# Placing the tiles that the dense matmuls read at multiples of 512 bytes of SBUF

## The chip, the core and the metric

The kernel runs on one core of one Trainium2 chip. The metric is the device time of one execution in microseconds (us), from the start to the end of the program on that core. In the profile the engines are called PE (TensorE, the matmuls), PEld (TensorE's loads of the stationary operand), DVE (VectorE), ACT (ScalarE), POOL (GpSimd) and SP (SyncE, which issues most of the DMAs).

A matmul here has a **moving** operand, which streams through the array column by column (up to 512 columns), and a **stationary** operand of 128 x 128, which is loaded ahead of it. In the rows of the trace `mm<-hH,wh` means: output tile `mm`, moving operand `hH`, stationary operand `wh`.

## The reference, cut to what matters

Two layers over 512 tokens with a model width of 1024, everything in float32:

```python
for layer in range(DEPTH):                     # DEPTH = 2
    h = rmsnorm(x, attn_norm[layer])
    proj = einsum('bsd,dc->bsc', h, w_in[layer])       # 6920 columns
    out_a = spatial_gating(...)                # 128 x 128 mixing matrices
    out_b = sliding_window_attention(...)      # 8 heads, window 128, rotary tables
    out_c = gated_deltanet(...)                # chunked recurrence, 4 heads
    merged = sum(sigmoid(gate_i) * (branch_i @ w_branch[layer, i]))   # 3 branches
    x = x + merged @ w_out[layer]
    h2 = rmsnorm(x, ffn_norm[layer])
    gu = h2 @ w_gate_up[layer]                 # 5632 columns
    x = x + (silu(gu[:2816]) * gu[2816:]) @ w_down[layer]
return rmsnorm(x, final_norm)
```

Nearly all the arithmetic is in the products with `w_in`, `w_branch`, `w_out`, `w_gate_up` and `w_down`. These are called the dense matmuls below. The rest (delta rule, attention, transposes) is made of many small matmuls.

## The kernel before

**Number format.** Each float32 operand of a dense matmul is split into a high part, rounded to the matmul format float32r, and a low part, the exact rest. A product is the sum of three matmuls: high x high, high x low, low x high. So there are tiles in pairs: `wh`, `wl` (weights), `hH`, `hL` (normed residual), `brH`, `brL` (branch outputs), `mH`, `mL` (merged branches), `aH`, `aL` (activations of the feed-forward). Each holds 4 bytes for every element.

**Weights.** `wload` fetches 512 KB of weights by DMA into `st` (two buffers), ACT rounds them into `wh`, DVE subtracts to get `wl` (three buffers each). One such load feeds 24 matmuls.

**Dense matmuls.** `fm_acc` takes a slice of 128 columns of `wh` or `wl` as the stationary operand and a whole tile of 512 columns of `hH`, `aH`, `brH` or `mH` (or the low part) as the moving one. `tm_group` has it the other way round: a slice of 128 columns of `hH` or `hL` is stationary and 512 columns of `wh` or `wl` move (264 columns for the projection of attention's keys and values, `wkv`).

**Order.** The class `Issue` writes the order of PE's instructions by a rough clock of its own: the dense matmuls form one long stream, and steps of the delta rule, attention and so on are put between them. The other engines' instructions are ordered by the scheduling layer. The function `layer` goes through key/value projection, the projections of the mixers with the delta rule and attention interleaved, gates and branches, the output projection, and the feed-forward (first gate and up: `hH`, `hL`; then down: `aH`, `aL`).

**Placement.** SBUF is handed out by pools, one after the other in each partition: `const` (constants such as `ones`, `ident`, masks), `lay` (small tiles of a layer), `base` (`hH`, `hL`, five scratch pages `rot`, `ms`, `rst`, `rep`), `wst` (`st`, `wh`, `wl`), and then the pools of the mixers (`mix`, pages of 2 KB) or of the feed-forward (`ffn`). Sizes are rounded up to 32 bytes. A tile's address is therefore the sum of all that stands ahead of it. As the program is built, these are the places of the operands, as the remainder of the address by 512 bytes:

| operands | pool | before | changed |
|---|---|---|---|
| `hH`, `hL` (8 tiles of 2 KB each) | `base` | 96 | 0 |
| `wh`, `wl` (3 buffers of 4 KB each) | `wst` | 224 | 0 |
| `aH`, `aL` | `ffn` | 224 | 0 |
| `brH`, `brL`, `mH`, `mL` | `mix` | 224 | 0 |
| the second half of the 264-wide weights | `wst` | 256 | 32 |
| `ones`, `ident`, `tri_le` | `const` | 288 | 64 |
| `dg` (in `rot`) | `base` | 96 | 0 |

The slices of 128 columns start at multiples of 512 bytes inside their tiles, so a slice has the remainder of its tile.

Of the kernel before, what the change touches and what calls it, by code (L numbers as in the profile page):

```python
# [10 lines left out]
F32 = mybir.dt.float32  # L11
# [7 lines left out]
P = 128  # L19
# [11 lines left out]
# chunk indices of the packed input projection  # L31
# [7 lines left out]
DENSE = 10  # L39
ORDER = "k z qv0 qv1 aq gv u"  # L40
# [7 lines left out]
class Issue:  # L48
    """Merges streams of work into one order for the tensor engine.

    A stream is a generator: it yields None where other streams may go on, or the name of an event to wait for.
    Of the streams whose last step should be through, the one of the lowest rank goes on.  When a step is
    through comes from a rough clock (us): every engine works off what it is given, and waits for operands."""
# [40 lines left out]
    def bank_free(self, tag, n):  # L94
        """when the next of the n banks of this tag can be written"""
        used = self.banks.setdefault(tag, [])
        return self.read.get(used[-n], 0.0) if len(used) >= n else 0.0
# [6 lines left out]
    def front(self, nc):  # L104
        """nc with engines that keep the clock"""
        issue = self

        class Engine:
            def __init__(self, name):
                self.name, self.eng = name, getattr(nc, name)  # L110

            def __getattr__(self, op):
                f = getattr(self.eng, op)

                def call(*args, **kw):
                    issue.note(self.name, op, args, kw)
                    return f(*args, **kw)  # L117

                return call

        class Front:
            vector, scalar, gpsimd, tensor, sync = (Engine(e) for e in ("vector", "scalar", "gpsimd", "tensor", "sync"))

        return Front
# [37 lines left out]
def hybrid_kernel(ctx, tc, x0, pos, wi, wkv, wb, wo, wg, wd, gn, convw, lngb, sguw, sgub,  # L162
# [20 lines left out]
    def pg(tag, name, shape=(P, T), dt=F32):  # L183
        """a page of 2 KB of the layer's pool; a tag's pages are handed out in program order"""
        return pools["mix"].tile(list(shape), dt, tag=tag, name=nm(name), bufs=PAGES[tag])
# [14 lines left out]
    def wload(src, n=1024, ahead=True):  # L200
        """f32 weights -> (high, low) parts, high rounded to float32r and low the exact rest"""
        st = wst.tile([P, 1024], F32, tag="st", name=nm("st"), bufs=2)
        hi = wst.tile([P, 1024], F32R, tag="wh", name=nm("wh"))
        lo = wst.tile([P, 1024], F32R, tag="wl", name=nm("wl"))
        issue.ahead = ahead
        with tc.high_priority() if ahead else nullcontext():
            nc.sync.dma_start(st[:, :n], src)
            nc.scalar.copy(hi[:, :n], st[:, :n])
            nc.vector.tensor_tensor(lo[:, :n], st[:, :n], hi[:, :n].bitcast(F32), ALU.subtract)
        issue.ahead = False  # L210
        return hi, lo

# [1 line left out]
    xp = tc.tile_pool(name="x0", bufs=1, reuse_waits="tile")  # L214
    x0p = xp.__enter__()
    gnt = cst([P, 2 * DEPTH + 1, KT], "gnt")
    nc.sync.dma_start(gnt, gn)
# [19 lines left out]
    # rows p, columns f  # L237
    ident = tri("ident", [[1, P]], 0, -1, ALU.is_equal)
    tri_le = tri("tri_le", [[1, P]], 0, -1, ALU.is_ge)      # f >= p
    tri_gt = tri("tri_gt", [[-1, P]], 0, 1, ALU.is_gt)      # p > f  # L240

    # blk[b][p, f] = 1 when p and f lie in one block of size b
# [11 lines left out]
    # lmt[b][i, j] = 1 when i and j share a block of 2b, j in its left half and i in its right one  # L254
# [7 lines left out]
    # additive masks of the attention band, columns [previous chunk | this chunk]  # L262
# [18 lines left out]
    def rope_tables():  # L281
        with tc.tile_pool(name="rope", bufs=1) as rp:
# [7 lines left out]
            ang = rp.tile([P, NCH, 8], F32, name="ang")  # L290
# [18 lines left out]
            w = rp.tile([P, NCH, 8], F32, name="w")  # L309
# [6 lines left out]
    def fm_acc(ps, w, off, xs, first, last):  # L316
        """ps[c, t] += sum over the k tiles of w[:, off + 128 i ...].T @ xs[i], operands as (high, low)"""
        wh, wl = w
        for i, (xh, xl) in enumerate(xs):
            sl = slice(off + i * P, off + (i + 1) * P)  # L320
            nc.tensor.matmul(ps, lhsT=wh[:, sl], rhs=xh, start=first and i == 0, stop=False)
            nc.tensor.matmul(ps, lhsT=wh[:, sl], rhs=xl, start=False, stop=False)
            nc.tensor.matmul(ps, lhsT=wl[:, sl], rhs=xh, start=False, stop=last and i == len(xs) - 1)
            yield
# [7 lines left out]
    def tm_group(srcs, width, xs):  # L332
        """four banks [128 tokens, width]: tokens by columns, k tiles in pairs; weights may be loaded already"""
        yield issue.bank_free("mm", 1)
        banks = [mm_bank() for _ in range(NCH)]
        for j, src in enumerate(srcs):
            wh, wl = src if isinstance(src, tuple) else wload(src, 2 * width)
            for c in range(NCH):
                tk = slice(c * P, (c + 1) * P)
                for kk in range(2):  # L340
                    xh, xl = xs[2 * j + kk]
                    sl = slice(kk * width, (kk + 1) * width)
                    o = banks[c][:, :width]
                    nc.tensor.matmul(o, lhsT=xh[:, tk], rhs=wh[:, sl], start=j == 0 and kk == 0, stop=False)
                    nc.tensor.matmul(o, lhsT=xh[:, tk], rhs=wl[:, sl], start=False, stop=False)
                    nc.tensor.matmul(o, lhsT=xl[:, tk], rhs=wh[:, sl], start=False, stop=j == 3 and kk == 1)
                yield
        return banks

# [6 lines left out]
    class Norm:  # L356
        """takes the residual tile by tile; gives the scaled operand in two parts and 1/rms"""

        def __init__(self, gi, final=False, split=KT - 1):
            """the squares of the tiles before split are added on GpSimd, the others on VectorE"""  # L360
# [25 lines left out]
        def finish(self):  # L386
# [4 lines left out]
            ms = base.tile([P, NCH], F32, tag="ms", name=nm("ms"), bufs=2)  # L391
            nc.vector.tensor_scalar(ms, ps[:, :NCH], 1.0 / D, EPS, ALU.mult, ALU.add)
            self.rst = base.tile([P, NCH], F32, tag="rst", name=nm("rst"), bufs=2)
# [16 lines left out]
    def layer(l, norm, first=None):  # L410
# [39 lines left out]
        # beta = sigmoid, g = -exp(a_log) * softplus(a + dt_bias)  # L450
# [26 lines left out]
        # 2 z (1 + p) + max(x, 0)  # L477
# [21 lines left out]
        def dn_conv(which, h, name):  # L499
            """2 silu(conv(projection)), feature-major"""  # L500
# [33 lines left out]
        class Delta:  # L534
            """two heads of the gated delta rule, in steps that leave the order of issue to the caller"""
# [15 lines left out]
            def decay(self):  # L551
                """decay^T[j, i] = exp(sum of g over (j, i]) for i >= j"""
# [16 lines left out]
            def keys(self):  # L569
                """scaled k k^T and token-major keys"""  # L570
# [35 lines left out]
            def queries(self):  # L606
                """scaled q k^T, size of q, token-major values"""
# [36 lines left out]
            def solve(self, c):  # L644
                """U = (I + L)^-T by doubling of the diagonal blocks; Tm = U^T"""
# [55 lines left out]
            def scan(self):  # L701
                yield f"z{l}"
                for c in range(NCH):
# [5 lines left out]
                    # right side minus what the state holds already  # L709
# [42 lines left out]
                    # rms norm over the head, z gate  # L752
# [14 lines left out]
        def blocks(wk):  # L767
            """inverses of the 16 x 16 diagonal blocks of I + L, one block a partition"""
# [18 lines left out]
            # [(block, row), inverse or its transpose, (group, chunk, head), column]  # L787
# [8 lines left out]
        def gelu2(x):  # L796
            """x <- 2 gelu(x)"""
# [6 lines left out]
        def sgu_params():  # L804
            """causal mixing matrices and, per column c and row t, lnb[c] * sum_s W[t, s] + b[t]"""
# [30 lines left out]
        def sgu():  # L836
            """us <- 4 u * (W n + b), n the norm of v"""
# [44 lines left out]
        def rope(t, co, si, n, name):  # L882
            """t [P, n, 64], tables [P, n, 8]"""
# [8 lines left out]
        def attn_prep():  # L892
            """keys, then the queries chunk by chunk, feature-major"""
# [31 lines left out]
        def attn_pair(qk, qT, kT, c, a, jj):  # L925
            """two heads of key head a in chunk c; the result replaces the queries"""
# [53 lines left out]
        def to_branch(key, srcs, tags, events):  # L980
            """token-major pieces [feature tile][chunk] -> feature-major (high, low) tiles"""
# [198 lines left out]
def _tiles_fm(w):  # L1180
    """[K, C] -> [C/128, 128, K] : per 128 columns, partition p holds (k tile, column)"""
    K, C = w.shape
    return w.reshape(K // P, P, C // P, P).transpose(2, 1, 0, 3).reshape(C // P, P, K)


def _tiles_tm(w):
    """[K, C] -> [K/256, 128, 2 C]"""
# [66 lines left out]
```

## Time and profile before

| | |
|---|---|
| device time, median of 3 runs | 1800.73 us (1800.56 to 1803.62) |
| span of the profiled execution, first to last instruction | 1798.6 us |
| PE busy in the profiled execution | 1768.7 us of the span (98%) |
| PEld, DVE, ACT, POOL busy | 1451.9, 886.1, 634.7, 399.2 us |
| mean granted TensorE clock | 0.996 of full speed |

The page of the profile gives no time of the profiled execution other than its span, so the median is 2.1 us above it. Matmuls overlap in the array: one that the rows show as 0.39 us long is followed by the next after 0.23 us, so the distance from start to start is what a matmul costs PE, and the length in the row is not.

### The profile page before, as it was taken

How to read it: one execution, taken by the hardware profiler on the slowest of the kernel's cores; microseconds unless marked ns; L12 is line 12 of the kernel's file. 1: busy time of each engine (PE TensorE's matmuls, PEld its weight loads, DVE VectorE, ACT ScalarE, POOL GpSimd, SP SyncE). 2: the span in 40 equal slices, each digit the busy share in tenths (PEclk: the TensorE clock that was granted, in tenths of full speed). 3: DMA queues.
4: the chain of work that ended last, by engine and by line, in shares of the span. 5: the costliest groups of instructions: out<-in, count | busy, mean ns of one | idle time of the engine just before them, and what ended most of it. 6: DMA issues, size and time to landing. Idle time of an engine off the chain costs nothing.

```text
span 1798.6 us, 22123 instructions
## 1 busy us (share of the span) xinstructions
PE 1768.7 (98%) x8458; PEld 1451.9 (81%) x8458; DVE 886.1 (49%) x1756; ACT 634.7 (35%) x1155; POOL 399.2 (22%) x399
## 2 busy tenths in 40 slices
PE   7999999999999999999999999999999999999996
PEld 6888878888888888888888888888888888888885
DVE  7695775454443333333267858654444433333222
ACT  6454454322333222222244435432223322222221
POOL 4413111011223333310043121010222233333011
PEclk9999999999999999999999999999999999999998
DMA  4232112222352222234332311122234522223331
GB/s 156 96 97 72 36 36 77 94 94 94 108 170 97 97 96 94 94 115 134 114 104 93 100 48 36 54 82 94 84 104 135 187 94 94 94 94 93 96 97 65
DMA packets 55784, 171.84 MB, mean 96 GB/s; under 512 B 8000, under 2 KB 8256, under 8 KB 55680
## 3 DMA queue, kind: packets, MB, share of 16 engines
q1 hardware_dynamic: 54432, 167.04, 28.5%
q0 software_dynamic: 1248, 3.41, 0.7%
q8 instruction: 66, 1.08, 0.3%
q14 instruction: 38, 0.31, 0.1%
HBM read 159.41 MB, written 11.01 MB: 95 GB/s over the span
## 4 chain that ended last, share of the span: by engine, by line
PE 96%; DVE 2%; ACT 1%; issue 0%; POOL 0%; DMA 0%; DVEq 0%; SPq 0%; POOLq 0%; ACTq 0%
PE mm L117 85%; PE px L117 10%; DVE wl L117 0%; DVE xf L117 0%; DVE U L117 0%; DMA st<-in_wkv 0%; ACT wh L117 0%; POOL of L117 0%; DVE zg L117 0%; DVE sq L117 0%; DVE ys L117 0%; DVE Tm L117 0%; ACT sq L117 0%; POOL rst L117 0%; DVE hL L117 0%
## 5 line engine op out<-in xcount | busy, mean ns | idle before, releaser
L117 ACT CAST wh<-st 128x1024 fp32r<-128x1024 f32 (+2 forms) x288 | 295.8, 1027 | 814.3 <-PE mm L117 733.4
L117 PE MATMUL mm<-hH,wh 128*128 128x512 f32 x1344 | 538.3, 401 | 0.0
L117 PE MATMUL mm<-hH,wl 128*128 128x512 f32 x1344 | 530.4, 395 | 0.0
L117 PE MATMUL mm<-hL,wh 128*128 128x512 f32 x1344 | 530.2, 394 | 0.0
L117 DVE TENSOR_TENSOR wl<-st,wh 128x1024 fp32r<-128x1024 f32 (+2 forms) x288 | 355.2, 1233 | 184.3 <-ACT wh L117 174.4
L117 PEld LDWEIGHTS mm<-hH,wl 128*128 128x128 f32 x1344 | 252.9, 188 | 59.4
L117 PEld LDWEIGHTS mm<-hH,wh 128*128 128x128 f32 x1344 | 253.2, 188 | 58.5 <-issue 2.7
L117 PEld LDWEIGHTS mm<-hL,wh 128*128 128x128 f32 x1344 | 253.3, 188 | 56.5 <-issue 0.7
L117 PE MATMUL mm<-aH,wh 128*128 128x512 f32 x352 | 137.0, 389 | 0.0
L117 PE MATMUL mm<-aH,wl 128*128 128x512 f32 x352 | 137.0, 389 | 0.0
L117 PE MATMUL mm<-aL,wh 128*128 128x512 f32 x352 | 136.9, 389 | 0.0
L117 POOL TENSOR_TENSOR gt<-gt,gt 128x512 f32<-128x512 f32 x32 | 48.9, 1528 | 306.8 <-DVE gt L117 306.8
L117 POOL TENSOR_TENSOR s<-s,rep 128x512 f32<-128x512 f32 x44 | 77.3, 1756 | 167.5 <-ACT s L117 167.5
L117 POOL TENSOR_TENSOR aL<-s,aH 128x512 fp32r<-128x512 f32 x44 | 76.5, 1738 | 163.4 <-ACT aH L117 163.4
L117 PE MATMUL mm<-wh,hH 128*128 128x512 f32 (+1 forms) x256 | 101.9, 398 | 7.2 <-ACT hH L117 7.2
L117 DVE TENSOR_TENSOR s<-mm,s 128x512 f32<-128x512 f32 x44 | 30.4, 692 | 155.6 <-PE mm L117 148.8
L117 DVE TENSOR_TENSOR s<-mm,rep 128x512 f32<-128x512 f32 x44 | 30.4, 692 | 143.9 <-PE mm L117 140.0
L117 PE MATMUL mm<-wh,hL 128*128 128x512 f32 (+1 forms) x256 | 95.3, 372 | 0.7 <-DVE hL L117 0.4
L117 PE MATMUL mm<-wl,hH 128*128 128x512 f32 (+1 forms) x256 | 94.8, 370 | 0.0
L117 POOL TENSOR_TENSOR sq<-sq,sq 128x512 f32<-128x512 f32 x27 | 40.7, 1509 | 236.3 <-ACT sq L117 236.2
L117 DVE TENSOR_TENSOR gt<-mm,rep 128x512 f32<-128x512 f32 x48 | 33.1, 690 | 103.7 <-PE mm L117 103.7
L117 PEld LDWEIGHTS mm<-aH,wh 128*128 128x128 f32 x352 | 66.1, 188 | 13.9
(250 smaller groups left out, 2359.0 us busy)
## 6 DMA issues: line engine op xcount, KB each, us to landing
st<-in_wi SPq DMA_DIRECT2D x104, 512.0 KB, 3.2
st<-in_wg SPq DMA_DIRECT2D x88, 512.0 KB, 3.3
st<-in_wd SPq DMA_DIRECT2D x32, 512.0 KB, 3.5
st<-in_wb SPq DMA_DIRECT2D x24, 512.0 KB, 3.3
st<-in_wo SPq DMA_DIRECT2D x16, 512.0 KB, 3.4
xscr<-xt SPq DMA_DIRECT2D x24, 256.0 KB, 2.0
st<-in_wd SPq DMA_DIRECT2D x16, 384.0 KB, 3.1
xt<-xscr SPq DMA_DIRECT2D x16, 256.0 KB, 2.7
```

What stands on the lines that cost most here:

```text
L117: return f(*args, **kw)
```

## The change

Five edits, all of placement:

- a tile `pad` of 72 floats (288 bytes) is put into `const` behind `gnt`; nothing reads or writes it;
- `ms` and `rst` (two buffers of 16 bytes each, 32 with rounding) move from `base` to `lay`, ahead of `base`;
- in the rotary tables `ang` is the tile `inv` itself, and `w` is the tile `nh`, which gives up two small tiles at the end of SBUF.

With these the pool `base` starts at 25600 (before: 25184) and `wst` with the weights at 78848 for `wh` (before: 78560), both multiples of 512. The comments and docstrings of the file are left out too, which moves the line numbers by a few.

```diff
+PAD = 72
...
     gnt = cst([P, 2 * DEPTH + 1, KT], "gnt")
+    cst([P, PAD], "pad")
...
             inv = rp.tile([P, NCH, 8], F32, name="inv")
...
-            ang = rp.tile([P, NCH, 8], F32, name="ang")
+            ang = inv
             nc.vector.tensor_tensor(ang, inv, pf.unsqueeze(2).broadcast_to([P, NCH, 8]), ALU.mult)
...
-            w = rp.tile([P, NCH, 8], F32, name="w")
+            w = nh
...
-            ms = base.tile([P, NCH], F32, tag="ms", name=nm("ms"), bufs=2)
+            ms = lay.tile([P, NCH], F32, tag="ms", name=nm("ms"), bufs=2)
             nc.vector.tensor_scalar(ms, ps[:, :NCH], 1.0 / D, EPS, ALU.mult, ALU.add)
-            self.rst = base.tile([P, NCH], F32, tag="rst", name=nm("rst"), bufs=2)
+            self.rst = lay.tile([P, NCH], F32, tag="rst", name=nm("rst"), bufs=2)
```

On each of the five engines the built program has the same instructions in the same order with the same waits as before; only tile names (`inv` for `ang`, `nh` for `w`) and addresses differ.

## Rows read from the trace of the kernel before

**Rows 1.** The page: span, busy time of the engines, chain that ended last.

```profile
span 1798.6 us, 22123 instructions
...
PE 1768.7 (98%) x8458; PEld 1451.9 (81%) x8458; DVE 886.1 (49%) x1756; ACT 634.7 (35%) x1155; POOL 399.2 (22%) x399
...
PE 96%; DVE 2%; ACT 1%; issue 0%; POOL 0%; DMA 0%; DVEq 0%; SPq 0%; POOLq 0%; ACTq 0%
```

**Rows 2.** Waits: who <- for whom: us in total, times, longest us.

```profile
ACT wh L117 <- PE mm L117: 733.4, 230, 6.7
...
PE mm L117 <- ACT hH L117: 7.2, 2, 5.7
PE px L117 <- DVE sq L117: 3.6, 2, 2.4
```

**Rows 3.** PE's timeline in gate and up, layer 0: start us, length us, instruction.

```profile
639.67 0.40 PE L117 MATMUL mm<-hL,wh 128*128 128x512 f32 x1
...
641.05 0.40 PE L117 MATMUL mm<-hL,wh 128*128 128x512 f32 x1
641.30 0.40 PE L117 MATMUL mm<-hH,wl 128*128 128x512 f32 x1
...
641.76 0.39 PE L117 MATMUL mm<-hL,wh 128*128 128x512 f32 x1
```

**Rows 4.** PE's timeline in the down projection, layer 0.

```profile
819.62 0.39 PE L117 MATMUL mm<-aH,wh 128*128 128x512 f32 x1
...
821.66 0.39 PE L117 MATMUL mm<-aH,wh 128*128 128x512 f32 x1
```

**Rows 5.** PE's timeline in the z projection, layer 0 (weights move).

```profile
55.24 0.39 PE L117 MATMUL mm<-wh,hL 128*128 128x512 f32 x1
...
57.10 0.39 PE L117 MATMUL mm<-wl,hH 128*128 128x512 f32 x1
```

**Rows 6.** Groups by operation and form: xcount, busy us, mean ns, idle before.

```profile
L117 PE MATMUL mm<-hH,wh 128*128 128x512 f32 x1344 | 538.3, 401 | 0.0
...
L117 PE MATMUL mm<-aH,wh 128*128 128x512 f32 x352 | 137.0, 389 | 0.0
...
L117 PE MATMUL mm<-wh,hH 128*128 128x512 f32 x192 | 81.8, 426 | 0.0
...
L117 PE MATMUL mm<-brH,wh 128*128 128x512 f32 x192 | 74.8, 389 | 0.0
...
L117 PE MATMUL mm<-mH,wh 128*128 128x512 f32 x128 | 49.8, 389 | 0.0
...
L117 PE MATMUL mm<-wh,hH 128*128 128x264 f32 x64 | 20.1, 314 | 7.2 <-ACT hH L117 7.2
```

**Rows 7.** PE's timeline around a full float32 matmul: x2 is its two passes.

```profile
538.19 1.02 PE L117 MATMUL px<-dg,ones 128*128 128x512 f32 x2
```

**Rows 8.** The tile `dg`: duration ns min/median/max of its matmuls.

```profile
L117 PE MATMUL px<-dg,ones x10: 592/593/1192, 26.3 to 1786.8; 128*128 128x512 f32 x10
```

**Rows 9.** PE's timeline in the first projection, 264 columns, near the program's start.

```profile
9.84 0.42 PE L117 MATMUL mm<-wh,hH 128*128 128x264 f32 x1
...
12.26 0.42 PE L117 MATMUL mm<-wh,hL 128*128 128x264 f32 x1
```

**Rows 10.** PE's timeline in the same projection some microseconds later.

```profile
18.93 0.29 PE L117 MATMUL mm<-wl,hH 128*128 128x264 f32 x1
...
20.14 0.28 PE L117 MATMUL mm<-wh,hL 128*128 128x264 f32 x1
```

**Rows 11.** Stretches: bounds, length, engines' busy us (xcount), clock, DMA share, GB/s.

```profile
150.00:250.00 100.00, 98.50 (x648) 82.43 (x647) 73.36 (x275) 49.23 (x149) 20.61 (x36) 1.00 0.13 43
560.00:740.00 180.00, 180.00 (x776) 145.97 (x775) 61.46 (x65) 51.42 (x64) 58.08 (x33) 1.00 0.29 94
1000.00:1150.00 150.00, 146.60 (x886) 121.05 (x887) 109.89 (x378) 72.26 (x212) 26.07 (x41) 1.00 0.17 54
```

**Rows 12.** Groups in the stretch 150 to 250 us.

```profile
L117 PE MATMUL mm<-wh,hH 128*128 128x512 f32 x40 | 17.4, 436 | 0.0
...
L117 PE MATMUL mm<-hH,wh 128*128 128x512 f32 x12 | 5.3, 440 | 0.0
```

## The prediction

> **What bounds the kernel now.** I read the page first: PE is busy for 98% of a span of 1798.6 us, and 96% of the chain that ended last is PE [rows 1]. The view of waits says the same from the other side: ACT waits 733.4 us in total until PE gives a weight buffer back, while PE's longest sums of waiting are 7.2 and 3.6 us [rows 2]. So weights are never late in the long stretches, and the time is the number of matmuls times the distance from one start to the next. That distance is what the timeline gives; the lengths in its rows overlap.
>
> There are three distances for a dense matmul of 512 columns, all at a granted clock of 1.00, the level of 2.4 GHz [rows 11]. In gate and up (moving `hH`, stationary `wh`) nine steps take 641.76 - 639.67 = 2.09 us, 232.2 ns each [rows 3]. In the down projection (moving `aH`, stationary `wh`) nine take 2.04 us, 226.7 ns each [rows 4]. In the z projection (moving `wh`, stationary `hH`) eight take 1.86 us, 232.5 ns each [rows 5]. The array's own need is 512 / 2.4 = 213.3 ns. So each dense matmul pays 13 to 19 ns on top. The instruction is the same in all three; what differs is where the operands lie. `hH` is at remainder 96 by 512, all other dense operands at 224. Two operands at 224: 226.7. One at 96, in either role: 232.
>
> **What the surplus is not.** It is no fixed cost of a matmul. In the first projection, 264 columns wide, eleven steps near the start take 2.42 us, 220.0 ns each [rows 9]. That is exactly 264 / 1.2, so I read it as the lower level of the clock, with nothing on top, with the same operands and the same weight loads. Later the same matmuls go at 1.21 / 10 = 121.0 ns [rows 10] where 264 / 2.4 is 110.0. A full float32 matmul takes two cycles a column: its two passes start 1.02 - 0.59 = 0.43 us apart [rows 7, 8], where 1024 cycles are 426.7 ns, though its moving tile `dg` is also at 96. So the surplus appears only where one 4-byte element a cycle is asked for at 2.4 GHz: the read of the operands limits, not the array.
>
> The sizes suggest how. 226.7 ns are 544 cycles = 17 x 32. If a read comes in lines of 128 bytes (32 elements, 32 cycles each), 2048 bytes that start at remainder 96 of 128 touch 17 lines and not 16. The 264 columns (1056 bytes) touch 9 lines, 288 cycles, 120.0 ns: the row says 121.0. Lines of 64 bytes would give 33 x 16 = 528 cycles, 220 ns, too little; lines of 256 bytes 9 x 64 = 576, 240 ns, too much. This is an estimate from four spacings, not something that a row shows directly. The 5.5 ns more for a pair at 96 and 224 would then be the two reads getting in each other's way.
>
> A rule of the Trainium skill stands against a part of this. The page "TensorE: Matmul & The Clock Gate", section "Step-by-step: what each phase is for", says that PE reads the moving and the stationary operand by two independent ports, so that loading the next weights takes nothing from the running matmul. By that rule the z projection, whose moving operand is at 224, should go at the 226.7 ns of the down projection; its row says 232.5, so here the measurement decides, and the place of the stationary operand counts too.
>
> **The change part by part.** No instruction, wait or DMA is added, removed or moved; `pad` is never touched. The shared tiles of the rotary tables are some 20 operations of 32 elements on DVE, in the order as before: nothing. `ms` and `rst` are four elements wide: nothing. The sum is therefore the number of dense matmuls times the change of their spacing.
>
> The new spacing at remainder 0: 16 lines are 512 cycles, 213.3 ns, and the fixed part that the float32 pair shows (430 against 426.7 ns) adds 3. I take 216. The bounds are 213.3 (nothing fixed left) and 226.7 (the best that a row shows for this instruction). The value is nearer the lower end because both float32 passes and the slow stretch come within 3 ns of the array's need as soon as the reads aren't the limit.
>
> - Gate, up, gates of branches, and the projections with moving `hH`, `hL`: 3 x 1344 = 4032 matmuls [rows 6], 16.2 ns each: 65.3 us.
> - Projections with moving weights: 3 x 192 = 576, 16.5 ns each: 9.5 us.
> - Moving `aH`, `brH`, `mH` and their low parts: 3 x (352 + 192 + 128) = 2016, 10.7 ns each: 21.6 us.
> - The 264-wide ones: 3 x 64 = 192. At 0 and 32 they still touch 9 lines; 121 to 120 ns, taken as nothing. At most 192 x 8 = 1.5 us.
>
> Together 96.4 us. Against it: in 150 to 250 us and in 1000 to 1150 us PE is idle for 1.5 and 3.4 us [rows 11], between steps of the delta rule and attention that wait for other engines. There dense matmuls fill the waits, and faster ones fill less. About 3 x (40 + 12) = 156 of them lie in the first stretch [rows 12], 156 x 16 = 2.5 us, and by length 3.7 us in the second. I take half of these 6 us as given back: 3 us (bounds 0 and 6). In the feed-forward nothing else comes near: in 180 us DVE works 61, ACT 51, POOL 58, and the DMAs are at a share of 0.29 [rows 11]. At 216 ns for 232 that grows by 7%. If this cover were gone, the next late thing would be `wl`, which DVE makes out of `st`.
>
> The span becomes 1798.6 - 96.4 + 3 = 1705.2 us. The median of the runs is 2.1 us above the profiled span, so 1707 us.
>
> **The rivals.**
>
> 1. *Only the pair counts.* What the rows show directly is that equal remainders do better than unequal ones. If the other 13 ns belong to any full-rate read (544 cycles could also be 512 plus one stolen cycle for each 16 bytes of a 512-byte weight load), all dense matmuls go at 226.7: 4032 x 5.5 + 576 x 5.8 = 25.5 us, 1775 us. For it: it needs nothing that no row has shown. Against it: 264 columns would then need 264 + 32 = 296 cycles, 123.3 ns, and the row says 121.0.
> 2. *Placement does nothing.* `hH` differs from the others also in when it runs and where in SBUF it lies, and that could be the cause; then 1801 us. Against it: `wh` and `hH` swapped give the same spacing. The Trainium skill's page "SBUF — State Buffer" has a rule by which this would be so: "Operand start alignment" asks only for a multiple of the element size (and says that it speaks of legality, not of speed), and "Specifications (TRN2)" gives lines of 16 bytes; every tile here starts at a multiple of 32 before the change. By that the three spacings should be one; the rows have two, 5.5 ns apart.
> 3. *Slower.* With all operands at 0 the moving read and the weight load, which begins as a matmul starts, begin at the same place of a line and of any interleave. If that makes them collide each time, every dense matmul takes what the worst step in gate and up takes, 641.30 - 641.05 = 0.25 us, say 240 ns: 4032 x 7.8 + 576 x 7.5 + 2016 x 13.3 = 63 us more, 1863 us. It decides from a mean spacing of 230.6 ns on, today's mean over all 6624. Against it: two operands at 224 begin alike too, and are the fastest.
> 4. *In between*, the line effect for the moving operand alone with some collisions left, spacing about 221: some 65 us, 1736 us.
>
> **How the numbers follow.** My forecast 0.55, rival 1 0.20, rival 2 0.10, rival 3 0.10, rival 4 0.05. The forecast's own range is 1689 (213.3 ns, 18 us less) to 1727 (219 ns). To leave out no more than 2 in 10 the range has to reach to rival 1: 1689 to 1778. Differences under 0.2% can't be told from none. Faster holds the forecast and rivals 1 and 4: 0.80; the same 0.10; slower 0.10.
>
> **What would show it.** In the changed kernel's timeline, steps of 216 ns in gate and up, down and z alike; if down stays at 226.7 and gate and up comes to it, it is rival 1. The 264-wide steps should stay at 120 to 121 and the float32 pair at 0.43. PE's idle time in the two delta stretches should grow by no more than some 3 us each. I am wrong if the 13 ns at equal remainders don't depend on the place, or if remainder 0 brings collisions of its own.

## The result, and the profile after

The changed kernel takes 1778.83 us (median of 4 runs, 1778.37 to 1779.13), the kernel before 1800.67 us in the same series. The ratio is 0.9875 (95% interval 0.9861 to 0.9889): 1.2% faster, 22 us and not the 94 us that I forecast. The time lies 0.8 us outside my range, next to rival 1 (only the pair counts, 1775 us).

The page of the changed kernel, its span, busy times and chain, as in [rows 1]:

```profile
span 1776.7 us, 22123 instructions
...
PE 1747.9 (98%) x8458; PEld 1451.2 (82%) x8458; DVE 885.9 (50%) x1756; ACT 633.8 (36%) x1155; POOL 397.3 (22%) x399
...
PE 96%; DVE 2%; ACT 1%; issue 0%; POOL 0%; DMA 0%; DVEq 0%; SPq 0%; POOLq 0%; ACTq 0%
```

The same instructions, the other engines as busy as before to within 2 us, PE 21 us less. So only what a matmul costs PE has changed. PE's timeline in gate and up, layer 0, to be held against [rows 3] (start us, length us, instruction):

```profile
639.64 0.39 PE L118 MATMUL mm<-hH,wh 128*128 128x512 f32 x1
...
641.91 0.39 PE L118 MATMUL mm<-hL,wh 128*128 128x512 f32 x1
```

Ten steps in 2.27 us, 227.0 ns; before they were 232.2. In the down projection, against [rows 4]:

```profile
819.61 0.39 PE L118 MATMUL mm<-aH,wl 128*128 128x512 f32 x1
...
821.65 0.39 PE L118 MATMUL mm<-aH,wl 128*128 128x512 f32 x1
```

Nine steps in 2.04 us, 226.7 ns, as before to the digit, although all its operands went from remainder 224 to 0. The full float32 pair, against [rows 7], is unchanged too:

```profile
533.34 1.02 PE L118 MATMUL px<-dg,ones 128*128 128x512 f32 x2
```

The long pieces of the chain that ended last say it for whole stages (start us, length us, what). This is the feed-forward of layer 1, gate and up and then down, before (first line) and now:

```profile
1424.13 356.07 PE mm L117 x1545
...
1408.09 350.25 PE mm L118 x1545
```

That is 230.5 ns a matmul before and 226.7 now.

### The profile page after: what moved, and what is told of

Same layout as the page of the kernel before. It is cut to its first block, busy times and chain, and to the rows that moved or that the text cites. A ratio compares the mean times of both kernels' runs of the same rounds, so it can differ in the third digit from the quotient of the medians.

```text
span 1776.7 us, 22123 instructions
## 1 busy us (share of the span) xinstructions
PE 1747.9 (98%) x8458; PEld 1451.2 (82%) x8458; DVE 885.9 (50%) x1756; ACT 633.8 (36%) x1155; POOL 397.3 (22%) x399
## 4 chain that ended last, share of the span: by engine, by line
PE 96%; DVE 2%; ACT 1%; issue 0%; POOL 0%; DMA 0%; DVEq 0%; SPq 0%; POOLq 0%; ACTq 0%
PE mm L118 86%; PE px L118 10%; DVE wl L118 0%; DVE xf L118 0%; DVE U L118 0%; DMA st<-in_wkv 0%; ACT wh L118 0%; POOL of L118 0%; DVE zg L118 0%; DVE sq L118 0%; DVE Tm L118 0%; DVE ys L118 0%; ACT hH L118 0%; ACT pr L118 0%; ACT sq L118 0%
## 5 line engine op out<-in xcount | busy, mean ns | idle before, releaser
L118 PE MATMUL mm<-hH,wh 128*128 128x512 f32 x1344 | 532.2, 396 | 0.0
L118 PE MATMUL mm<-hH,wl 128*128 128x512 f32 x1344 | 524.0, 390 | 0.0
L118 PE MATMUL mm<-hL,wh 128*128 128x512 f32 x1344 | 523.3, 389 | 0.0
```

## The experiments

Two theories at the start. **Theory 1**: a dense matmul is slow when its two operands have different remainders, and the place itself is of no account. **Theory 2**: the place counts, a multiple of 128 or 512 is good. Spacings below are from start to start in PE's timeline of the run named.

**Each half of the change alone.** The first kernel moves `ms` and `rst` and leaves the pad out, so that every operand lies at 224; the second has the pad and leaves `ms` and `rst` where they were, so that `hH`, `hL` lie at 384 and the rest at 0.

```diff
 # e1_move_only: the changed kernel without
-    cst([P, PAD], "pad")
 # e2_pad_only: the changed kernel with
-            ms = lay.tile([P, NCH], F32, tag="ms", name=nm("ms"), bufs=2)
+            ms = base.tile([P, NCH], F32, tag="ms", name=nm("ms"), bufs=2)
-            self.rst = lay.tile([P, NCH], F32, tag="rst", name=nm("rst"), bufs=2)
+            self.rst = base.tile([P, NCH], F32, tag="rst", name=nm("rst"), bufs=2)
```

> The change without its pad: ms and rst in the layer's pool, so that all operands of the dense matmuls lie at remainder 224 by 512, none at 0. Theory 1 (only the pair counts: what matters is that the moving and the stationary operand have the same remainder): every dense matmul at 226.7 ns, time as the changed kernel, 1779 us. Theory 2 (the place itself counts: a multiple of 512, or of 128, is what helps): the gate and up projection doesn't come down to 226.7, and the time lies above 1785 us, up to 1801.

Measured: 1778.92 us, ratio 0.9879 (0.9864 to 0.9894). Gate and up:

```profile
639.74 0.39 PE L117 MATMUL mm<-hH,wh 128*128 128x512 f32 x1
...
641.78 0.39 PE L117 MATMUL mm<-hH,wh 128*128 128x512 f32 x1
```

Nine steps in 2.04 us, 226.7 ns, with every operand at 224.

> The change with its pad alone (ms and rst back ahead of the weights): hH and hL at remainder 384, weights and all other operands at 0, every one a multiple of 128; the difference of the pair is 128 as in the kernel before. Theory 1 (pair): gate and up stay at 232 ns, the rest at 226.7, time as before, 1801 us. Theory 2 (place): all operands are at multiples of 128, so 226.7 everywhere and 1779 us.

Measured: 1801.33 us, ratio 1.0001 (0.9992 to 1.0011). Gate and up:

```profile
639.74 0.39 PE L118 MATMUL mm<-hL,wh 128*128 128x512 f32 x1
...
641.83 0.39 PE L118 MATMUL mm<-hL,wh 128*128 128x512 f32 x1
```

Nine steps in 2.09 us, 232.2 ns, as in [rows 3], with every operand at a multiple of 128. Theory 1 stands, theory 2 has fallen: the whole gain comes from moving `ms` and `rst`, which takes 128 bytes out from between `hH` and the weights. The pad, which brings the multiples of 512, does nothing. (Both kernels keep the shared tiles of the rotary tables; the second shows that these give nothing either.)

**Which differences cost.** In the feed-forward's own pool gaps can be put between the activations, so that one run holds six differences between moving and stationary operand.

```diff
             act = []
+            place = 0
             for i in range(KF):
+                want = [[32, 64, 96], [128, 160, 192]][l][i // 8]
+                if want != place:
+                    fp.tile([P, (want - place) % 512 // 4], F32, tag=f"gap{i}", name=nm("gap"))
+                    place = want
```

> The changed kernel with small gaps between the activations of the feed-forward, so that in the down projection the moving operand lies off the stationary one by 32, 64, 96 bytes (layer 0: tiles 0 to 7, 8 to 15, 16 to 21) and by 128, 160, 192 (layer 1), by 512. Theory 1 (pair): more than 226.7 ns at 128 (about 232), and at each other difference a spacing of its own; 44 us per layer of down projection grow by 1 us for each 5 ns on a third of it. If the pair matters only by 128 or 256: multiples of 128 read differently from the rest. Theory 2 (place): multiples of 64 or 128 at 226.7 or lower, the others higher.

> As the sweep before, with differences of 224, 256, 288 bytes (layer 0) and 320, 384, 448 (layer 1). Theory 1 (pair): 384 about 232 ns, as hH against the weights in the kernel before (96 - 224). 256 tells whether the pattern repeats within 512: 226.7 if it repeats by 256, more if not. Theory 2 (place): 256 and 384 at 226.7.

Measured: 1785.7 and 1782.72 us (one run each). One stretch of 24 matmuls (23 steps) at a difference of 32 and one of 64, then 128, all of the first sweep:

```profile
795.15 0.39 PE L118 MATMUL mm<-aH,wh 128*128 128x512 f32 x1
...
800.51 0.40 PE L118 MATMUL mm<-aH,wl 128*128 128x512 f32 x1
800.75 0.40 PE L118 MATMUL mm<-aH,wh 128*128 128x512 f32 x1
...
806.02 0.39 PE L118 MATMUL mm<-aH,wl 128*128 128x512 f32 x1
...
1672.09 0.39 PE L118 MATMUL mm<-aH,wh 128*128 128x512 f32 x1
...
1677.43 0.39 PE L118 MATMUL mm<-aH,wl 128*128 128x512 f32 x1
```

5.36, 5.27 and 5.34 us, or 233, 229 and 232 ns a step. And 256 in the second sweep:

```profile
800.22 0.40 PE L118 MATMUL mm<-aH,wh 128*128 128x512 f32 x1
...
805.44 0.39 PE L118 MATMUL mm<-aH,wl 128*128 128x512 f32 x1
```

5.22 us, 227 ns. All differences, each from the first and last start of one such stretch (18 matmuls for 96, 192, 288 and 448):

```
difference, bytes    32    64    96   128   160   192   224   256   288   320   384   448
ns a step           233   229   234   232   234   234   233   227   233   229   232   233
```

0 and 256 are best, 64 and 320 next, 128 and 384 alike, 192 and 448 alike: the pattern repeats by 256 bytes, and none of these differences goes below 226.7. In this sweep the weights always lie at 0, so a rule for the place of the moving operand would read the same. For 0 and 128 bytes the other kernels tell the two apart (equal at 224 or at 0: 226.7; 96 with 224 or 384 with 0: 232.2); the other differences but 256 were measured with the weights at 0 alone. That 256 is as good as 512 was then tried on the whole kernel, with a gap of 256 bytes between the pool of `hH` and the weights.

```diff
-    cst([P, PAD], "pad")
...
+    wst.tile([P, 64], F32, tag="gap", name="gap", bufs=1)
```

> The change without its pad, and 256 bytes between the pool of hH, hL and the weights: hH, hL at remainder 224, weights and the rest at 480 by 512. The pair rule with a period of 256, as the sweep showed it: gate and up at 226.7 to 227 ns, time as the changed kernel, 1779 us. If 512 is the period: gate and up above 229 ns, 1790 us or more.

Measured: 1779.02 us (one run), in the range of the changed kernel's own runs. Added up from each start to the next in the trace, its 4032 matmuls with moving `hH`, `hL` take 925.7 us; in the changed kernel they take 925.6.

**What the other 13 ns are.** Theory A: a fixed toll per matmul, by the load of its stationary operand. Theory B: in proportion to the columns. Theory C: my lines. In the down projection the matmuls were cut by columns (all but the first and last of an output tile):

```diff
+    CUTS = [[(0, 256), (256, 512)], [(0, 384), (384, 512)]]
...
+                for c0, c1 in [(0, T)] if st_ or sp else parts:
+                    nc.tensor.matmul(ps[:, c0:c1], lhsT=a[:, sl], rhs=x[:, c0:c1], start=st_, stop=sp)
```

> The changed kernel, where in the down projection all but the first and last matmul of an output tile are cut by columns: into 256 + 256 in layer 0 and 384 + 128 in layer 1. Nothing else changes. Theory A (the 13.3 ns that are left at equal remainders are a fixed toll of one load of the stationary operand on the stream, 32 cycles for its 512 bytes): 256 columns take 106.7 + 13.3 = 120 ns, 384 take 173 ns; layer 0 grows by 512 x 13.3 ns = 7 us. Theory B (a read at full rate runs at 16/17 of the array's pace, in proportion to the columns): 113.3 and 170.0 ns; layer 0 doesn't grow. Theory C (lines of 128 bytes, as I predicted; fallen already for 512 columns): no surplus at remainder 0, 106.7 + 3 ns. In all, 128 columns are bound by the load at about 112 ns, so layer 1 grows by some 30 us.

Measured: 1816.9 us (one run), as 1779 + 7 + 30 would have it. Pairs of 256 columns in layer 0 (a row is one pair, two matmuls, each with a load of its own):

```profile
799.76 0.40 PE L118 MATMUL mm<-aL,wh 128*128 128x256 f32 x2
...
800.96 0.40 PE L118 MATMUL mm<-aH,wh 128*128 128x256 f32 x2
```

Five pairs in 1.20 us, 120.0 ns a matmul: 288 cycles, 256 + 32, where 512 columns take 512 + 32. Fixed, not in proportion (113.3), and not lines (106.7 + 3). The pairs of 384 + 128 in layer 1:

```profile
1700.02 0.45 PE L118 MATMUL mm<-aH,wh 128*128 128x384 f32 x2
...
1701.16 0.45 PE L118 MATMUL mm<-aL,wh 128*128 128x384 f32 x2
```

Four in 1.14 us, 285 ns a pair. Theory A's 173 + 112 makes 285, theory B's 170 + 112 makes 282. The starts don't show the two parts: in the trace the 128 columns start 227 ns after the 384, and the next 384 follow 59 ns later. So this layer agrees with A, but it is layer 0 that decides.

The load of the stationary operand was then made narrower, in a kernel that leaves out most of the down projection's terms for a part of its output.

```diff
+        n = (64, 32)[len(down_calls) // (3 * KT)]
...
+                m = P if st_ or sp else n
+                nc.tensor.matmul(ps[:m, :], lhsT=a[:, lo:lo + m], rhs=x, start=st_, stop=sp)
```

> The changed kernel, where in the down projection all but the first and last matmul of an output tile load only 64 (layer 0) or 32 (layer 1) of the 128 columns of the stationary operand, so that a part of the output gets only two of its 66 terms. Theory A (toll of the load, one cycle for each 16 bytes of it): 213.3 + 6.7 = 220.0 ns and 213.3 + 3.3 = 216.7 ns, some 8 us less in all, 1770 us. A toll by the load as such, whatever its size, or theory B (rate of the moving read): 226.7 ns in both, 1779 us.

Measured: 1783.02 us (one run), more and not less. With 64 columns in layer 0:

```profile
799.63 0.39 PE L118 MATMUL mm<-aH,wh 128*64 128x512 f32 x1
...
801.94 0.39 PE L118 MATMUL mm<-aL,wh 128*64 128x512 f32 x1
```

Ten steps in 2.31 us, 231 ns (229.8 over all of that layer, 231.6 with 32 columns). The loads did get shorter; the view of the tile `aH` (min/median/max ns) has

```profile
L118 PEld LDWEIGHTS mm<-aH,wh x352: 107/133/188, 764.2 to 1761.2; 128*64 128x64 f32 x80, 128*32 128x32 f32 x80, 128*128 128x128 f32 x16
```

107 and 133 ns for 188. So the toll doesn't follow the size of the load, and that half of theory A has fallen. Why the spacing grows instead, by 3 and 5 ns, isn't shown; no theory had that.

**Two bytes instead of four.** The operands of the down projection as pairs of bfloat16:

```diff
-                ah = fp.tile([P, T], F32R, tag=f"aH{i}", name=nm("aH"))
+                ah = fp.tile([P, T], BF16, tag=f"aH{i}", name=nm("aH"))
...
-                    w = wload(wd[l, m, :, k0 * P:k1 * P], (k1 - k0) * P)
+                    w = wload(wd[l, m, :, k0 * P:k1 * P], (k1 - k0) * P, dt=BF16)
```

> The changed kernel with the operands of the down projection (activations and weights, high and low parts) as pairs of bfloat16 and not of float32r: half the bytes in both reads, the same number of matmuls and columns; the result is a little less exact. If the surplus comes from reading 4-byte elements at full rate (theories A and B alike), it shrinks or goes: by A 220 ns (16 cycles for 256 bytes), without any surplus 213 to 216 ns: 1056 matmuls, 7 to 11 us less, 1768 to 1772 us. If it is a toll that each matmul pays whatever its bytes: 226.7 ns, 1779 us.

Measured: 1767.73 us, ratio 0.9812 (0.9795 to 0.9828).

```profile
819.70 0.38 PE L119 MATMUL mm<-aH,wl 128*128 128x512 bf16 x1
...
821.85 0.38 PE L119 MATMUL mm<-aH,wh 128*128 128x512 bf16 x1
```

Ten steps in 2.15 us, 215 ns (215.8 over all of the down projection): the toll is gone but for some 2 ns. The format changes more than the bytes of the moving read, though: the rows of the load fall too, from 0.19 us to 0.10.

```profile
790.34 0.10 PEld L119 LDWEIGHTS <-wl 128*128 128x128 bf16 x1
```

A short load alone doesn't remove the toll (107 ns at four bytes kept it), but bytes of either read and the way of loading were not changed one at a time. Then all dense matmuls in that form (`F32R` defined as bfloat16, the casts between the two dropped), once with all operands at 0 and once with 128 bytes between `hH` and the weights:

```diff
-F32R = mybir.dt.float32r
+F32R = mybir.dt.bfloat16
...
 # in the second kernel alone
+    wst.tile([P, 32], F32, tag="gap", name="gap", bufs=1)
```

> The changed kernel with every operand of a dense matmul as a pair of bfloat16 tiles, all at remainder 0: the same number of matmuls and columns, a less exact result. The down projection alone came to 216 ns in this form. If the toll belongs to 4-byte operands: 216 ns everywhere, 6624 x 10.7 ns = 71 us less than the changed kernel, of which the delta stretches may give back some: 1708 to 1715 us. If the down projection was a special case: more than 1730 us.

> The kernel with every operand as a pair of bfloat16 tiles, and a gap of 128 bytes between the pool of hH, hL and the weights, so that this pair lies 128 bytes apart as in the kernel before. If the cost of unequal remainders comes from two reads that together ask for too much (4-byte elements at 2.4 GHz), it is gone at 2 bytes: gate and up at 216 ns, the time of the kernel without the gap. If the pair rule is one of places alone: gate and up 5 ns longer, 4608 x 5 = 23 us more than without the gap.

Measured: 1705.5 us, ratio 0.9468 (0.9454 to 0.9483), and 1708.03 us, ratio 0.9478 (0.9463 to 0.9494); the intervals overlap. The first lies 2.5 us below the range expected of it. Gate and up of the second, with the operands 128 bytes apart:

```profile
619.98 0.38 PE L118 MATMUL mm<-hH,wh 128*128 128x512 bf16 x1
...
621.92 0.38 PE L118 MATMUL mm<-hH,wh 128*128 128x512 bf16 x1
```

Nine steps (one record, at 620.4, is missing) in 1.94 us, 215.6 ns. At two bytes 128 bytes of difference cost nothing. Other differences were not tried with 512 columns: if the pattern counts elements and not bytes, its period at two bytes is 128 bytes, and this test would miss it. The 264-wide steps speak against that, if faintly: the halves of their weights lie at 0 and 16 bytes in the first kernel and at 128 and 144 in the second, off `hH`, and in layer 1 all go at 112 to 113 ns. These two are the fastest kernels of this study, but they buy that with the number format, and so don't replace the change.

**Is the extra cost of unequal remainders per matmul too?** The cut into 256 + 256 in both layers, activations 128 and 32 bytes off:

```diff
+    CUTS = [[(0, 256), (256, 512)], [(0, 256), (256, 512)]]
...
+            fp.tile([P, (32, 8)[l]], F32, tag="gap", name=nm("gap"))
```

> The changed kernel with the down projection's matmuls cut into 256 + 256 columns, and the activations 128 bytes (layer 0) and 32 bytes (layer 1) off the weights by 512. At equal remainders 256 columns took 120.0 ns, the same toll of 13.3 ns as 512. If the extra cost of unequal remainders is paid per matmul too: 120 + 5.6 and 120 + 6.6 ns. If it grows with the columns: 120 + 2.8 and 120 + 3.3 ns.

Measured: 1786.75 us (one run), and neither. At 128 bytes (layer 0) and at 32 (layer 1):

```profile
799.79 0.40 PE L118 MATMUL mm<-aH,wh 128*128 128x256 f32 x2
...
800.97 0.40 PE L118 MATMUL mm<-aH,wl 128*128 128x256 f32 x2
...
1699.90 0.40 PE L118 MATMUL mm<-aH,wh 128*128 128x256 f32 x2
...
1701.07 0.40 PE L118 MATMUL mm<-aH,wl 128*128 128x256 f32 x2
```

From the first to the last row of each are five pairs: 1.18 and 1.17 us, 118 and 117 ns a matmul (118.7 and 116.7 over the whole layers), both under the 120.0 of equal remainders. At 32 bytes the surplus grows with the columns: about 24 cycles for 256 and 48 for 512. At 128 bytes it is about 29 and 45, neither fixed nor in proportion. At equal remainders it is 32 cycles for either. So equal remainders pay for 512 columns, and at 256 they are the worse choice, by 1 and 3 ns.

## Why the prediction was wrong

*What bounds the kernel* was right: PE's spacing, with nothing else near. The saving landed in the span one for one, and PE's idle time in the delta stretches hardly moved (1.5 and 3.6 us for the 1.5 and 3.4 of [rows 11]; the first numbers after the stretch are its length and PE's busy time):

```profile
150.00:250.00 100.00, 98.49 (x649) 82.52 (x648) 74.21 (x278) 48.68 (x148) 19.53 (x34) 1.00 0.14 45
...
1000.00:1150.00 150.00, 146.44 (x895) 120.89 (x895) 105.53 (x374) 71.76 (x214) 27.28 (x44) 1.00 0.16 52
```

*The step that failed* is "The new spacing at remainder 0: ... I take 216". It measured 226.7. Below it lay the lines of 128 bytes: four spacings fitted them, but a fixed 32 cycles fitted 512 columns just as exactly. By lines, going from 224 to 0 saves one line of 17, 13 ns; the down projection went there and stayed at 226.7. And 256 columns at 0 take 120.0 ns where eight lines are 106.7. Either refutes the lines.

*"It is no fixed cost of a matmul"* was the error of reasoning behind it. I read the 220.0 ns of [rows 9] as the lower clock. The view of stretches gives 1.00 there, but that trace has no record of the clock before 12.8 us, so no row showed the level. The changed kernel's trace bears the reading out: its granted clock is 0.50, the level of 1.2 GHz, from 24.1 to 27.5 us, and the same steps there, followed by a stretch of that time (length, busy us of the engines, clock, DMA share, GB/s), are

```profile
24.29 0.42 PE L118 MATMUL mm<-wh,hH 128*128 128x264 f32 x1
...
26.05 0.42 PE L118 MATMUL mm<-wh,hL 128*128 128x264 f32 x1
...
24.20:26.20 2.00, 2.00 (x11) 2.00 (x10) 1.15 (x6) 0.94 (x4) 1.02 (x1) 0.50 0.36 147
```

eight steps in 1.76 us, 220.0 ns. So nothing is added at the lower clock; I took that to exclude any fixed cost. The cut into 256 columns shows a cost at the upper clock that is the same per matmul for 256 and 512 columns.

And I used the 121.0 of [rows 10] against rival 1, which needed 123.3. That was too fine a reading: those steps have operands of unequal remainders, and at 256 columns unequal ones come out at 117 to 119, below equal ones. In the changed kernel one half of these weights lies at the remainder of `hH`, the other 32 bytes off; by the starts in layer 1 the halves take 122.1 and 121.2 ns. So 123.3 isn't reached at equal remainders either: with moving weights the 32 cycles don't hold exactly.

*The terms.* The 2016 matmuls with both operands at 224: 21.6 us forecast; by adding up the distances from each start to the next in both traces, 460.0 us became 459.5, so 0.5 measured. The 4032 with moving `hH`, `hL`: 65.3 forecast; 946.1 us became 925.6, so 20.5, of the 22.2 that rival 1 gave them. The 576 with moving weights: 9.5 forecast, 3.3 by rival 1, 1.2 measured (142.7 to 141.5). Their spacing at equal remainders is 228 in the z projection and 230 to 231 in the delta stretches; why it stays above 226.7, these runs don't show. The 264-wide ones: nothing forecast and nothing measured (121.7 ns before and after in layer 1). The three together are 22.2 us, and the span fell by 21.9. Of the give-back of 3 us nothing shows.

*Rival 1* was the right one, for the pair and nearly for the size, 1775 against 1778.8, and I gave it 0.20. That `hH` and `wh` swapped between the roles gave one spacing [rows 3 to 5] speaks for a rule of pairs, but my forecast had that part too. On the 13 ns, where the two differ, those rows are silent: 96 and 224 leave the same remainder by 128, so by lines as by a fixed toll each 512-wide matmul had the same 13 ns. With nothing to tell them apart the two should have had like chances. *Rival 3* (equal places collide) is excluded for 512 columns by all runs at equal remainders. *Rival 2* is excluded by the two halves of the change.

The Trainium skill's page "TensorE: Matmul & The Clock Gate", section "Step-by-step: what each phase is for", says that PE reads the moving and the stationary operand by two independent ports, so that the load of the next weights takes nothing from the running matmul. For 4-byte operands the traces disagree, as the spacing depends on where the two lie to each other (227 to 234 ns); for 2-byte ones they agree as far as tried (215.8 ns at a difference of 0 and of 128 bytes).

*Left open:* what the 32 cycles are, and which read pays them. They come with 4-byte operands at 2.4 GHz, per matmul, for 256 as for 512 columns, and a narrower load doesn't lower them. A float32r matmul without a load of its own wasn't tried. Nor is it shown how the two reads get in each other's way at unequal remainders; the runs show when they do, and what it costs.

## What to carry to other kernels

Where PE is the bound, measure the distance between starts, stage by stage, before anything else: two spacings for one kind of instruction mean that something other than the instruction differs. For float32r matmuls of 512 columns, give moving and stationary operands the same remainder by 256 bytes: here that was worth 5 ns of 232 where activations move and 2 ns where weights move. The alignment itself buys nothing. At 256 columns the rule turns round, and with bfloat16 operands the one difference tried cost nothing. When a surplus fits a formula, look for a second formula that fits too, and ask which row of the trace could tell them apart under the same conditions; if none can, the two get like chances.

## What the runs showed that I had not expected

- A float32r matmul with moving activations takes 226.7 ns for 512 columns and 120.0 ns for 256 at equal remainders, 32 cycles of 2.4 GHz over its columns; on bfloat16 operands 512 columns take 215 to 216 ns.
- The place of the moving operand relative to the stationary one matters with a period of 256 bytes, for float32r and 512 columns: 227 ns at 0 and 256, 229 at 64 and 320, 232 to 234 elsewhere.
- A narrower stationary operand (64 or 32 columns) shortens its load from 188 to 133 and 107 ns in the rows and makes the matmul's spacing longer, 229.8 and 231.6 ns for 226.7.
